# A two-layer encoder trunk on one core: the last gate with tokens on partitions, casts queued ahead of spreads, and five more tiles of u in a borrowed region

## The chip, the core and the metric

The kernel runs on one core of one Trainium2 chip. The core has a matrix engine (TensorE, PE in the views, its weight loads PEld), a vector engine (VectorE, DVE), a scalar engine (ScalarE, ACT), GpSimd (POOL), and SyncE (SP), whose queue issues nearly all transfers. The metric is the device time of one execution in microseconds; the kernel counts as changed if its median moves by more than the measurement can tell.

## What is computed

The input is x, 256 tokens of 1024 features, with two layers. Each layer has a mixer (layer 0: Mamba-2 SSD, layer 1: retention), an expert network of 128 x 128 experts (PEER), and a gated per-layer input. A final RMS norm ends it. The last parts, cut from the reference:

```
h = h + peer_ffn(rms_norm(h, ffn_norm[i]), peer_w_q[i], peer_keys[i], peer_u[i], peer_v[i])
g = jax.nn.sigmoid(rms_norm(h, ple_norm[i]) @ ple_gate[i])
h = h + g * (p[i] @ ple_proj[i])
...
return rms_norm(h, final_norm)
```

In `peer_ffn` every token picks, per head, 16 of the experts by two top-16 searches over 128 keys each; a picked expert's row of u is multiplied with the token, passed through gelu, weighted by a softmax gate and multiplied with its row of v. The kernel computes the products for all 16384 experts densely and multiplies by a gate matrix that is zero where an expert was not picked.

## The kernel before

**Activations and weights.** The residual is kept as `hT`, features on partitions, tokens along the free axis, eight chunks of 128 features (`hch`). Products are made in a split form: a weight tile of 128 x 1024 is loaded into a `raw` buffer (four of them, `raws`), cast by ScalarE into `wh` (lines 136 and 532), and the rest is subtracted into `wl` by VectorE or GpSimd (139, 535); `wh` and `wl` have two buffers each. Activations are split the same way into X tiles. A product is then three passes: wh with the high part, wh with the low part, wl with the high part.

**The weight pipeline.** `makers` is the list of all weight tiles in order. `begin()` issues the transfer of the next one; `prepare()` emits its cast and, unless `late`, its subtraction; `get()` hands out the tile for this step, prepares the next and begins one more. `ahead()` prepares a tile early, leaving its subtraction to the next `get()`. Whatever is emitted later on an engine runs later there: each engine works its queue in the order of emission.

**A dense product.** `dense` goes over eight k-steps of 128 input features; in each it takes a tile, lets the stream bring its activations up to date (`Stream.before`: gain copies by ScalarE, line 332, low parts by VectorE, line 337), emits 24 matmuls of 256 tokens (line 206) and then `fill`s in pieces of other work, as many as the plan of the step says. With `ends=2` the last two k-steps are done bank by bank (`close`, line 221), so that the four banks of PSUM end one after the other. The norm's division is applied to the product: squares on ScalarE (`q`, `Q`, line 349) are added on GpSimd (351, 353); `t` sums them by a matmul with ones (256), a root is taken on VectorE and GpSimd (263, 265), a diagonal made (275), and `s` spreads it over the partitions by two matmuls (282), copied by ScalarE (361). The plans FIRST_SSD, FIRST_RET, FIRST_Q and FIRST_PLE say after which k-step each of these letters is emitted.

**Retention.** Projections, then scores, mixing and a group norm per head, whose pieces stand in RET_ORDER (q: squares, b: sum and diagonal, c: spread and scaling); RET_GATE says how many pieces follow each k-step of the two gate projections. RET_LO lists the tiles whose subtraction GpSimd does.

**PEER.** Two query projections (the second one's subtractions on GpSimd), with eight small transfers of the normed activations after each of the first two steps (`q_move`), from which the X tiles for u are split (`q_fill`). Then 128 tiles of u: each is loaded as four transfers into a row buffer, transposed by VectorE in 32 x 32 blocks (527), cast and split, and multiplied in 24 matmuls (1289, 1290, 1293). The row buffer is one of four slots at offset 16384 of the region `H` that will later hold the experts' activations, as long as i < UEND, and a `raw` buffer after that; the transposed tile is always a `raw` buffer. During the first 60 tiles VectorE also does the selection (`pump`). From the tile where the selection ends, the gate matrix is built for four tokens at a time, 64 groups: `g_hot` makes one-hots on VectorE (1195, 1197), `g_lo` a low part on ScalarE (1203), `g_mm` multiplies them (1209), `g_apply` stores or multiplies the result into H (1219, 1223). `g_slot`, once per tile, emits the matmuls of two ready groups, the one-hots of a next group (two where `since % 8 == 0` and it lags) and the low parts. After the 128 tiles of u, 128 tiles of v are multiplied with H, now with H as the stationary operand and 512 features as the moving one (1315); `peer` ends with the transposes of the result into the residual and the projection of p (1353), evacuated by ScalarE (1357).

**The last stage.** `ple(1, ...)` makes the gate product, divides (364), tanh (1408), multiplies (1384) and adds (1388) into `hT`; `turned_out` transposes 16 chunks back to tokens on partitions (1398), squares and sums them (1401), and the end of `trunk` takes the root (1468 to 1470), scales (1475) and stores four pieces (1476):

```
for j in range(2):
    for tb in range(2):
        o = raws.tile([P, D], F32, name="raw")[:, :512]
        c = slice(512 * j, 512 * j + 512)
        dve.scalar_tensor_tensor(o, ot[2 * j + tb], v[:, 1, tb:tb + 1], gfin[:, c], op0=OP.mult, op1=OP.mult)
        (sp, act)[tb].dma_start(out[0, tb * P:(tb + 1) * P, c], o)
```

## Time and profile before

| | |
|---|---|
| median of three executions | 2146.82 us (2146.73 to 2147.22) |
| the profiled execution | 2147.86 us, its span 2145.3 us |
| mean granted TensorE clock | 0.996 |
| busy share of the span | PE 98%, PEld 91%, DVE 73%, ACT 57%, POOL 36% |
| transfers | 370.24 MB, mean 173 GB/s |
| query projections, tiles of u, tiles of v, layer 1 | about 1288, 1340 and 1750 us from the span's start to the start of each |
| last matmul of the last gate | 2131.75 us |

The span runs from the first to the last instruction; the execution's own time is 2.56 us longer. In the views, "L206" is line 206 of the kernel; `out<-in` names what is written and read; times are microseconds from the span's start, then the duration. A bracket at a row's end is the idle time of the engine before it and what ended it. Matmul durations overlap.

### The profile page before, as it was taken

How to read it: one execution, taken by the hardware profiler on the slowest of the kernel's cores; microseconds unless marked ns; L12 is line 12 of the kernel's file. 1: busy time of each engine (PE TensorE's matmuls, PEld its weight loads, DVE VectorE, ACT ScalarE, POOL GpSimd, SP SyncE). 2: the span in 40 equal slices, each digit the busy share in tenths (PEclk: the TensorE clock that was granted, in tenths of full speed). 3: DMA queues.
4: the chain of work that ended last, by engine and by line, in shares of the span. 5: the costliest groups of instructions: out<-in, count | busy, mean ns of one | idle time of the engine just before them, and what ended most of it. 6: DMA issues, size and time to landing. Idle time of an engine off the chain costs nothing.

```text
span 2145.3 us, 39601 instructions
## 1 busy us (share of the span) xinstructions
PE 2112.3 (98%) x15013; PEld 1959.3 (91%) x15013; DVE 1559.6 (73%) x2645; ACT 1218.8 (57%) x2136; POOL 772.1 (36%) x359
## 2 busy tenths in 40 slices
PE   8999999999999999999999999999999999999997
PEld 8999999999999888888898999999999998888887
DVE  7787688979998555555695457888799975555556
ACT  5675444558887444444554444445688864444445
POOL 0001378876776000000143215788767740000001
PEclk9999999999999999999999999999999999999999
DMA  6424687645555655666655456765555565555553
GB/s 199 147 90 130 206 195 188 175 131 156 156 157 170 199 192 193 194 195 191 217 156 179 121 176 186 189 186 138 161 155 158 152 186 194 196 193 191 195 191 118
DMA packets 219574, 370.24 MB, mean 173 GB/s; under 512 B 24240, under 2 KB 163192, under 8 KB 219384
## 3 DMA queue, kind: packets, MB, share of 16 engines
q1 hardware_dynamic: 218920, 366.93, 57.4%
q8 instruction: 117, 1.92, 0.4%
q10 hardware_dynamic: 464, 0.79, 0.1%
q14 instruction: 73, 0.60, 0.1%
HBM read 364.48 MB, written 1.05 MB: 170 GB/s over the span
## 4 chain that ended last, share of the span: by engine, by line
PE 44%; DVE 2%; issue 1%; POOL 1%; ACT 1%; DMA 1%; SPq 0%; DVEq 0%; POOLq 0%; ACTq 0%
PE ps L1315 16%; PE ps L206 7%; PE m L1289 5%; PE m L1293 5%; PE m L1290 5%; PE ps L913 2%; PE g L1209 1%; DMA raw<-in_peer_u 1%; PE g L1017 0%; DVE wl L139 0%; POOL wl L139 0%; DVE raw L527 0%; PE g L865 0%; POOL wl L535 0%; SPq L524 0%
## 5 line engine op out<-in xcount | busy, mean ns | idle before, releaser
L139 DVE TENSOR_TENSOR wl<-raw,wh 128x1024 fp32r<-128x1024 f32 x404 | 503.6, 1248 | 397.2 <-ACT wh L136 396.9
L136 ACT CAST wh<-raw 128x1024 fp32r<-128x1024 f32 x428 | 449.4, 1052 | 470.5 <-PE ps L1315 358.7
L535 POOL TENSOR_TENSOR wl<-raw,wh 128x1024 fp32r<-128x1024 f32 x256 | 618.1, 2415 | 203.3 <-ACT wh L532 189.2
L1289 PE MATMUL m<-X,wh 128*128 128x256 f32 x2048 | 508.7, 286 | 1.3 <-ACT wh L532 1.3
L1315 PE MATMUL ps<-wh,X 128*128 128x512 f32 x2048 | 507.1, 389 | 0.0
L1290 PE MATMUL m<-X,wh 128*128 128x256 f32 x2048 | 502.3, 283 | 0.0
L1315 PEld LDWEIGHTS ps<-wh,X 128*128 128x128 f32 x2048 | 384.1, 188 | 79.6
L1289 PEld LDWEIGHTS m<-X,wh 128*128 128x128 f32 x2048 | 392.5, 192 | 2.6 <-ACT wh L532 2.3
L1290 PEld LDWEIGHTS m<-X,wh 128*128 128x128 f32 x2048 | 392.7, 192 | 0.0
L206 PE MATMUL ps<-X,wh 128*128 128x256 f32 x2368 | 330.3, 288 | 3.3 <-ACT wh L136 1.2
L351 POOL TENSOR_TENSOR arena<-arena 128x512 f32<-128x512 f32 x15 | 24.1, 1610 | 809.6 <-ACT arena L349 800.5
L206 PEld LDWEIGHTS ps<-X,wh 128*128 128x128 f32 x2368 | 302.0, 194 | 9.5 <-DVE arena L364 1.9
L1293 PE MATMUL m<-X,wl 128*128 128x256 f32 x2048 | 288.1, 283 | 2.1 <-POOL wl L535 2.1
L532 ACT CAST wh<-raw 128x1024 fp32r<-128x1024 f32 x256 | 266.4, 1041 | 25.4 <-DVE raw L527 16.6
L1315 PE MATMUL ps<-wl,X 128*128 128x512 f32 x1024 | 274.7, 389 | 0.0
L1293 PEld LDWEIGHTS m<-X,wl 128*128 128x128 f32 x2048 | 264.0, 192 | 3.8 <-POOL wl L535 3.5
L1315 PEld LDWEIGHTS ps<-wl,X 128*128 128x128 f32 x1024 | 192.2, 188 | 40.0
L1229 ACT ACTIVATE arena<-m 128x256 f32<-128x256 f32 (+15 forms) x248 | 82.0, 331 | 229.6 <-PE m L1293 229.4
L527 DVE STREAM_TRANSPOSE raw<-raw 128x1024 f32<-128x1024 f32 x144 | 179.0, 1243 | 42.4 <-DMA raw<-in_peer_u 31.0
L206 PE MATMUL ps<-X,wl 128*128 128x256 f32 x1184 | 175.1, 284 | 2.3 <-POOL wl L139 1.3
L527 DVE STREAM_TRANSPOSE raw<-arena 128x1024 f32<-128x1024 f32 x112 | 138.0, 1235 | 30.1 <-POOL wl L535 22.3
L206 PEld LDWEIGHTS ps<-X,wl 128*128 128x128 f32 x1184 | 156.4, 192 | 3.6 <-POOL wl L139 1.9
(269 smaller groups left out, 1969.4 us busy)
## 6 DMA issues: line engine op xcount, KB each, us to landing
raw<-in_peer_v SPq DMA_DIRECT2D x256, 512.0 KB, 4.3
raw<-in_peer_u SPq DMA_DIRECT2D x576, 128.0 KB, 3.1
arena<-in_peer_u SPq DMA_DIRECT2D x448, 128.0 KB, 3.2
raw<-in_ret_w_in SPq DMA_DIRECT2D x48, 512.0 KB, 3.9
raw<-in_ssd_w_in SPq DMA_DIRECT2D x41, 512.0 KB, 3.7
raw<-in_peer_w_q SPq DMA_DIRECT2D x32, 512.0 KB, 4.3
raw<-in_ssd_w_out SPq DMA_DIRECT2D x16, 512.0 KB, 3.8
raw<-in_ple_gate SPq DMA_DIRECT2D x16, 512.0 KB, 4.7
```

The source lines that it names most:

```text
L136: (cast or act.copy)(wh[:, :n], r[:, :n])
L139: (eng or dve).tensor_sub(wl[:, :n], r[:, :n], wh[:, :n].bitcast(F32))
L206: pe.matmul(self.t[n // 2][:, n % 2], w[:, n * P:(n + 1) * P], x, start=st, stop=sp_, skip_group_check=True)
L527: dve.transpose(t.rearrange("p (k b i) -> p b k i", k=8, b=4), r.rearrange("p (b k i) -> p b k i", k=8, b=4))
L532: act.copy(wh, t)
L535: pool.tensor_sub(wl, t, wh.bitcast(F32))
L913: pe.matmul(pss[j], abc[i][0][:, tb * P:(tb + 1) * P], abc[i][1][:, n * 512:(n + 1) * 512], start=kk == 0 and i == 0, stop=kk == 7 and i == 2)
L1229: act.activation(H[:, i, st:], ps[:, st:], AF.Gelu)
L1289: pe.matmul(last, wh[:, s], xh, start=k == 0, stop=False)
L1290: pe.matmul(last, wh[:, s], xl, start=False, stop=False)
L1293: pe.matmul(last, wl[:, s], xh, start=False, stop=k == KD - 1)
L1315: pe.matmul(sums[b], h[:, tb * P:(tb + 1) * P], w[:, n * 512:(n + 1) * 512], start=i == 0 and p == 0, stop=i == P - 1 and p == 2)
```

## The change

1. The last gate, projection and output are written as `ple_last`, with tokens on partitions: the activations are the stationary operand, 512 features the moving one. The residual is transposed within the gate (`turn`, after steps 1 and 2) and p's projection added to it; the norm's root is a scale per partition of the tanh, so there is no spread. The output is scaled by the final root in four pieces.
2. `spread` calls `ahead()` first, and the first step of retention's first projection does so too (`turned`).
3. FIRST_RET moves the letters Q, t, s and the first scaling one step later; RET_GATE moves the last sum of the group norm one step later; RET_LO gives tile 46 to VectorE.
4. The last tile of the second query projection is subtracted by VectorE; the activations for u are split one step earlier.
5. UEND goes from 56 to 61.
6. The second one-hot of a slot is emitted after `g_done`.

```diff
 NEG = -3.0e38
 GS = 4096.0
 PUMP = 1700
-UEND = 56
+UEND = 61
 HPOOL = (0, 1)
...
 RET_ORDER = """
     n0 m0 s1 q0 m1 s2 b0 c0 n1 s3 q1 m2 b1 n3 c1 n2 q2 m3 b2 c2 q3 b3 c3
 """.split()
-RET_GATE = (2, 2, 1, 2, 1, 2, 1, 2, 1, 2, 1, 2, 1, 2, 1, 0)
-RET_LO = (8, 22, 31, 33, 46, 48, 51)
+RET_GATE = (2, 2, 1, 2, 1, 2, 1, 2, 1, 2, 1, 2, 1, 2, 0, 1)
+RET_LO = (8, 22, 31, 33, 48, 51)
 FIRST_SSD = ('aq', 't', 'c', 's', '0', 'h', '1b', 'H')
-FIRST_RET = ('', 'qQ', '', 'cbt', 'das0', '', 'h1', 'H')
+FIRST_RET = ('', 'q', 'Q', 'cb', 't', 'das0', 'h1', 'H')
 FIRST_Q = ('q', 'Q', '', 't', 'sa', 'b', '', '')
 FIRST_PLE = ('', 'q', 'Q', '', 't', 's', '', '')
+FIRST_LAST = ('', 'qa', 'Qb', '', 't', '', '', '')
 HEADS = 8
 TOPK = 16
...
         def __init__(self, col):
             self.col, self.xs, self.n, self.src = col, [], 0, hch
+            self.turned = False
             self.sq, self.rb = view(12288, 4, 512), view(14336, T)
         def gain(self, c):
...
         def before(self, k):
+            if self.turned and not k:
+                ahead()
             while len(self.xs) < KD:
                 self.hi(len(self.xs))
             while self.n < min(k + 3, KD):
...
             self.sums.sum(self.sq[:, 0, :T])
             self.dg = self.sums.diag(D)
+        def roots(self):
+            self.sums = Sums()
+            self.sums.sum(self.sq[:, 0, :T])
+            r = self.sums.root(D)
+            self.rh = small.tile([P, 2], F32, name="rh", bufs=1)
+            dve.tensor_scalar(self.rh, r, 0.5, None, op0=OP.mult)
         def spread(self):
+            ahead()
             act.copy(self.rb, self.sums.spread(self.dg))
         def divide(self, dst, ps):
...
             for k in range(16):
                 weights(a["ret_w_out"][0], 0, D, k, k + 1, eng=pool if 48 + k in RET_LO else None)
         for g in range(2):
-            weights(a["peer_w_q"][l], g * D, (g + 1) * D, eng=pool if g else None)
+            for k in range(KD):
+                weights(a["peer_w_q"][l], g * D, (g + 1) * D, k, k + 1, eng=pool if g and k < KD - 1 else None)
         for i in range(P):
             makers.append(lambda l=l, i=i: u_maker(a["peer_u"][l], i))
         weights(a["peer_v"][l], 0, D, 0, P)
...
             if k < 2:
                 q_move(2 * k)
                 q_move(2 * k + 1)
-            if k in (4, 6):
-                xh, xl = split_x(xm[:, 2 * k - 8:2 * k - 4])
+            if k in (3, 5):
+                xh, xl = split_x(xm[:, 2 * k - 6:2 * k - 2])
                 xp.extend((xh[:, i], xl[:, i]) for i in range(4))
             return 0
...
             return len(gst["ready"]) > 1 or (gst["ready"] and gst["next"] == T // 4 and not gst["hot"])
-        def g_slot(n=1):
+        def g_new():
+            if gst["next"] < T // 4 and not bg and gst["next"] < gst["mms"] + 4:
+                gst["hot"].append((gst["next"], g_hot(gst["next"])))
+                gst["next"] += 1
+        def g_slot():
             if g_due():
                 for b, x in gst["ready"][:2]:
...
                     gst["mms"] += 1
                 gst["ready"] = gst["ready"][2:]
             lo, gst["hot"] = gst["hot"], []
-            while n and gst["next"] < T // 4 and not bg and gst["next"] < gst["mms"] + 4:
-                gst["hot"].append((gst["next"], g_hot(gst["next"])))
-                gst["next"] += 1
-                n -= 1
+            g_new()
             for b, x in lo:
                 g_lo(b, *x)
                 gst["ready"].append((b, x))
...
                     pump(PUMP)
                 else:
                     since += 1
-                g_slot(2 if since % 8 == 0 and T // 4 - gst["next"] > P - 5 - i else 1)
+                g_slot()
                 g_done(i)
+                if since % 8 == 0 and T // 4 - gst["next"] > P - 5 - i:
+                    g_new()
                 if cur is None and not open_():
                     cur = wsplit(0)
             last = mis.tile([P, 512], F32, name="m")[:, :T]
...
                 wh, wl = get()
                 st2 = finish(turned, COL["ple_norm"] + 8 * l)
             for w_, x_ in ((wh, 0), (wh, 1), (wl, 0)):
+                if l:
+                    for j in range(4):
+                        pe.matmul(pq[j], pts[x_][:, kk, j // 2 * P:(j // 2 + 1) * P],
+                                  w_[:, j % 2 * 512:(j % 2 + 1) * 512],
+                                  start=kk == 0 and w_ is wh and x_ == 0, stop=kk == 1 and w_ is wl)
+                    continue
                 for n in range(8):
                     pe.matmul(pq[n // 2][:, (n % 2) * T:(n % 2 + 1) * T], w_[:, n * P:(n + 1) * P], pts[x_][:, kk],
                               start=kk == 0 and w_ is wh and x_ == 0 and n % 2 == 0, stop=kk == 1 and w_ is wl,
...
+    def ple_last(st, pp):
+        pp = pp.rearrange("p (a b) t -> p a (b t)", a=4)
+        g, hp, og, o = (view(i, 4, 512) for i in (2560, 6144, 8192, 24576))
+        gfin, junk = view(16384, D), view(17408, 512)
+        fs = small.tile([P, 2, 2], F32, name="fs", bufs=1)
+        v = small.tile([P, 2, 2], F32, name="r2")
+        sp.dma_start(gfin, a["final_norm"].partition_broadcast(P))
+        def turn(tb):
+            for n in range(2):
+                ps = gps.tile([P, 512], F32, name="g")
+                for c in range(4):
+                    pe.transpose(ps[:, c * P:(c + 1) * P], hch[4 * n + c][:, tb * P:(tb + 1) * P], ident)
+                dve.tensor_add(hp[:, 2 * tb + n], ps, pp[:, 2 * tb + n])
+        sums = [acc.tile([P, 512], F32, name="ps") for _ in range(4)]
+        def mms(j, wh, wl, xh, xl, parts, start, stop):
+            t, n = slice(j // 2 * P, (j // 2 + 1) * P), slice(j % 2 * 512, (j % 2 + 1) * 512)
+            for i in parts:
+                pe.matmul(sums[j], (xh, xl, xh)[i][:, t], (wh, wh, wl)[i][:, n], start=start and i == 0,
+                          stop=stop and i == 2)
+        st.total = st.roots
+        plan = first(st, None, FIRST_LAST, (turn, 0), (turn, 1))
+        for k in range(KD - 2):
+            wh, wl = get()
+            st.before(k)
+            for i in range(3):
+                for j in range(4):
+                    mms(j, wh, wl, *st.xs[k], (i,), k == 0, False)
+            fill(plan(k))
+        steps = [get(k < KD - 1) + st.xs[k] for k in (KD - 2, KD - 1)]
+        for j in range(4):
+            mms(j, *steps[0], range(3), False, False)
+            mms(j, *steps[1], range(3), False, True)
+        def tanh(j):
+            act.activation(g[:, j], sums[j], AF.Tanh, scale=st.rh[:, j // 2:j // 2 + 1])
+        def total(j):
+            dve.tensor_mul(g[:, j], g[:, j], pp[:, j])
+            dve.tensor_add(g[:, j], g[:, j], hp[:, j])
+        def square(j):
+            act.activation(junk, g[:, j], AF.Square, scale=1.0 / 32, accum_out=fs[:, j // 2, j % 2:j % 2 + 1])
+        def gains(j):
+            dve.tensor_mul(og[:, j], g[:, j], gfin[:, j % 2 * 512:(j % 2 + 1) * 512])
+        def root(tb):
+            dve.scalar_tensor_tensor(v[:, 0, tb:tb + 1], fs[:, tb, 0:1], EPS, fs[:, tb, 1:2], op0=OP.add, op1=OP.add)
+            pool.tensor_tensor(v[:, 1, tb:tb + 1], v[:, 0, tb:tb + 1], mhalf[:, :1], op=OP.pow)
+        def store(j, eng, queue):
+            r = v[:, 1, j // 2:j // 2 + 1]
+            if eng is act:
+                act.activation(o[:, j], og[:, j], AF.Copy, scale=r)
+            else:
+                dve.scalar_tensor_tensor(o[:, j], g[:, j], r, gfin[:, j % 2 * 512:(j % 2 + 1) * 512],
+                                         op0=OP.mult, op1=OP.mult)
+            queue.dma_start(out[0, j // 2 * P:(j // 2 + 1) * P, j % 2 * 512:(j % 2 + 1) * 512], o[:, j])
+        assert D == 1024
+        tanh(0)
+        tanh(1)
+        total(0)
+        square(0)
+        tanh(2)
+        total(1)
+        square(1)
+        tanh(3)
+        total(2)
+        root(0)
+        square(2)
+        total(3)
+        square(3)
+        gains(0)
+        store(0, act, sp)
+        root(1)
+        gains(2)
+        gains(3)
+        store(2, act, act)
+        store(1, dve, sp)
+        store(3, act, sp)
     state = [st0]
...
+    ple_last(*state)
```

## Rows read from the trace of the kernel before

**Rows 1.** The page, part 1: busy time, share of the span, instructions.
```profile
PE 2112.3 (98%) x15013; PEld 1959.3 (91%) x15013; DVE 1559.6 (73%) x2645; ACT 1218.8 (57%) x2136; POOL 772.1 (36%) x359
```
**Rows 2.** Chain that ended last, 2090 to 2146: start, duration, what, instructions.
```profile
2090.77 8.23 PE ps L1315 x36
...
2101.87 1.76 PE ps L1341 x16
...
2106.51 14.39 PE ps L206 x120
```
**Rows 3.** TensorE's waits, whole span: for whom, total, times, longest.
```profile
PE m L256 <- POOL arena L293: 1.8, 1, 1.8
PE g L1209 <- DVE arena L1223: 1.7, 2, 0.8
...
PE ps L221 <- ACT wh L136: 1.4, 2, 0.7
PE ps L206 <- POOL wl L139: 1.3, 2, 0.7
...
PE ps L206 <- ACT wh L136: 1.2, 1, 1.2
PE ps L221 <- DVE wl L139: 1.0, 2, 0.5
...
PE m L256 <- POOL arena L353: 0.8, 1, 0.8
```
**Rows 4.** Timeline of the last stage, 2122 to 2146.
```profile
2131.48 0.63 ACT L1408 ACTIVATE arena<-arena 128x512 f32<-128x512 f32 x1 [0.81 <-DVE arena L364]
...
2131.75 0.40 PE L221 MATMUL ps<-X,wl 128*128 128x256 f32 x2
...
2137.62 0.38 ACT L1401 ACTIVATE arena<-m 128x256 f32<-128x256 f32 x1
...
2138.57 0.70 POOL L1470 TENSOR_TENSOR r<-r,mhalf 128x2 f32<-128x2 f32 x1 [4.71 <-DVE r L1469]
...
2140.63 1.40 DVE L1475 SCALAR_TENSOR_TENSOR raw<-m,r,arena 128x512 f32<-128x512 f32 x2
2140.75 1.67 ACTq L1476 DMA_DIRECT2D out<-raw  x2
```
**Rows 5.** Timeline of retention's second gate projection, 1210 to 1246.
```profile
1229.37 2.40 POOL L139 TENSOR_TENSOR wl<-raw,wh 128x1024 fp32r<-128x1024 f32 x1 [1.74 <-ACT wh L136]
...
1234.83 0.61 PE L256 MATMUL m<-ones,arena 128*128 128x1 f32 x4 [1.79 <-POOL arena L293]
```
**Rows 6.** Window behind that wait: each engine's busy time, then granted clock, DMA share, GB/s.
```profile
1235.80:1239.20 3.40, 3.40 (x18) 3.40 (x18) 1.04 (x1) 1.77 (x4) 1.66 (x2) 0.50 0.21 81
```
**Rows 7.** Timeline of retention's first projection: its evacuations.
```profile
1101.46 2.48 DVE L364 TENSOR_TENSOR arena<-ps,arena 128x512 f32<-128x512 f32 x4
```
**Rows 8.** Timeline of layer 1's second query projection, 1305 to 1352.
```profile
1329.47 8.12 POOL L139 TENSOR_TENSOR wl<-raw,wh 128x1024 fp32r<-128x1024 f32 x3 [1.39 <-ACT wh L136]
...
1330.38 2.60 DVE L195 TENSOR_TENSOR X<-arena,X 128x1024 fp32r<-128x1024 f32 x1 [6.08 <-DMA arena<-in_peer_u]
```
**Rows 9.** Chain of waits among layer 1's tiles of u, 1500 to 1565.
```profile
1502.50 4.55 DMA raw<-in_peer_u
...
1515.52 3.19 DMA raw<-in_peer_u
...
1544.20 0.93 PE g L1209 x16
```
**Rows 10.** Timeline of TensorE: low-part matmuls of tiles 54, 62 (layer 0), 54, 63 (layer 1).
```profile
444.56 1.12 PE L1293 MATMUL m<-X,wl 128*128 128x256 f32 x8
...
471.24 1.12 PE L1293 MATMUL m<-X,wl 128*128 128x256 f32 x8
...
1501.97 1.12 PE L1293 MATMUL m<-X,wl 128*128 128x256 f32 x8
...
1533.47 1.12 PE L1293 MATMUL m<-X,wl 128*128 128x256 f32 x8
```

More of the change, by code (lines that the diff above doesn't have):

```diff
@@ L1416, in g_evac @@
                 gated(2)
[L1418 to L1421 removed]
+        keys = view(30464, 4, 512)
+        for c4 in range(4):
+            key_load(1, c4, keys[:, c4])
         dense(st, g_evac, first(st, None, FIRST_PLE), ends=2)
[L1423 to L1436 removed]
@@ L1437, in ple @@
-        ot = [pool_.tile([P, 512], F32, name=n_) for pool_, n_ in ((gps, "g"), (gps, "g"), (mis, "m"), (mis, "m"))]
+        tiles = [pool_.tile([P, 512], F32, name=n_) for pool_, n_ in ((gps, "g"), (gps, "g"), (mis, "m"), (mis, "m"))]
+        for c4 in range(4):
+            key_turn(keys[:, c4], tiles[c4])
+        st2.turned = True
+        st2.copies = [(key_copy, c4, tiles[c4]) for c4 in range(4)]
+        st2.lo(0)
+        ready.append(ready.pop()())
+        st2.lo(1)
+        prepare(True)
@@ L1438, in ple @@
+        ready.append(ready.pop()())
         added(2)
-        turned_out(0)
         gated(3)
         added(3)
-        for b in range(1, 4):
-            turned_out(b)
-        return ot, fs, gfin
+        return st2
+    def ple_last(st, pp):
[72 more added lines that the diff above has]
+        store(3, act, sp)
```

50 lines of the change are left out of this document (4 added, 46 removed).

## The prediction

> **What bounds the kernel now.** I read the page first: TensorE is busy 98% of the span [rows 1], so the sum of its matmuls is a floor, and a change can win only in fewer TensorE microseconds, in its waits, or behind its last matmul. The chain of waits gives the price of a matmul by the distance of successive starts, not by the listed duration, which overlaps the next one: 120 matmuls of 256 columns in 14.39 us are 0.120 us each, 36 of 512 columns in 8.23 us are 0.229, a transpose is 1.76/16 = 0.11 [rows 2]. Third, TensorE's own waits [rows 3]: each is under 2 us, and the seven listed, 9.2 us in all, sit where this diff works. Last, the timeline of the end [rows 4]: the last matmul ends at 2131.75 + 0.40 = 2132.15 and the span at 2145.3, so 13.15 us pass with hardly any TensorE work.
>
> **The change, part by part.** Times are against the profiled execution, 2147.86 us (span 2145.3 and 2.56 around it); the median of the three runs is 1.04 lower.
>
> (a) *Last gate and projection.* The gate's 24 matmuls of 256 columns per k-step become 12 of 512: 8 x (24 x 0.1199 - 12 x 0.2286) = 1.08 us less; the projection's 48 become 24, 0.27 less; four spread matmuls at 0.11 go, 0.45 less [rows 2]. The 16 transposes that ran behind the gate now run inside it, 1.76 more. TensorE's stream is therefore level (-0.05), and narrow against wide is worth little. What counts is the end. In the close, TensorE waited for the last weight tile's cast and then its subtraction, 1.4 and 1.0 us over the two gates [rows 3] plus the restart of the pipeline, 1.53 a gate by the starts. In the last gate no spread copy stands ahead of that cast any more, but the cast still needs the buffer of the tile two before, and the subtraction queues on VectorE behind the wait for the root. I put the wait at 0.9, so -0.6.
>
> Behind the last matmul I walk the new order, with t = 0 at its end and durations of [rows 4]. Banks finish 6 x 0.229 = 1.37 us apart, so only the fourth counts. ScalarE is still squaring the second part until 0.2; tanh of the fourth takes 0.63, to 0.9. VectorE's two passes per part (1.40 for two) keep pace with the banks but finish the third part at 1.05; the fourth is done at 2.4. Its square with the sum read out is 0.38 for 256 columns plus the read; I estimate 0.75 for 512, to 3.2. A small VectorE sum, the power on GpSimd (0.70) and hand-overs reach 4.2. Two scaled copies on ScalarE at 0.63 end at 5.5, VectorE's own store beside them. From the last multiply's end before (2140.63 + 1.40 = 2142.03) to the end of the span were 3.27 us; two transfers queued on SP add 0.4. Sum: 9.1 instead of 13.15, -4.0. Part (a): **-4.7**; bounds -6 (no wait in the close, tail 8.3) and -2 (VectorE's four added 0.7 us adds push a weight subtraction late by 1, and the tail loses another 1.5).
>
> (b) *Cast ahead of the spread, gate of layer 0.* The same close, but the spread stays. With the cast ahead of it, the last cast starts when its buffer is free, 1.9 us into step 5, and the subtraction is late by about 0.45 instead of 1.53 in all: **-1.1**, bounds -1.5 and 0. At the query projections the same move finds no wait to remove: 0.
>
> (c) *Retention's first projection.* Step 2 waited 1.2 us (1.4 by the starts) for a cast queued behind four gain copies that wait for the residual; the sum of squares waited 0.8 for GpSimd [rows 3]. `ahead()` puts the cast first, and the sum moves to step 4, where the squares are long done. That makes TensorE up to 2.3 us earlier, but the scaled copies start at the end of step 5 instead of 4, and then VectorE, which needs 2.48 us for the four evacuations alone [rows 7], is late instead: TensorE waits for its banks some 0.8 longer. **-1.5**; bounds -2.3 and +0.5.
>
> (d) *Retention's gates.* GpSimd does a weight subtraction of 2.40 us, then two passes over the squares, and TensorE waits 1.8 for them [rows 3, 5]. Right behind that wait the granted clock reads 0.50, that is 1.2 GHz, for 3.4 us [rows 6]: 18 matmuls ran in it, where at 2.4 GHz 3.4 / 0.12 = 28 would, so it cost 10 x 0.12 = 1.2 more. The diff gives that subtraction to VectorE and lets the sum run a step later, after the evacuations; either is enough. Given back: the diagonal then waits for the power while ScalarE's queue holds the next cast, by my walk 0.65 us at the second output tile. The wait is 1.95 by the starts: -1.95 - 1.2 + 0.65 = **-2.5**; bounds -3.2 and +1 (the power behind the next GpSimd subtraction, 2.4 us, with a slow clock after it).
>
> (e) *Last tile of the second query projection on VectorE; splits of the moved activations one step earlier.* TensorE waits 1.3 us in two places, 0.8 each by the starts, for a GpSimd subtraction [rows 3], the last of three that took 8.12 instead of 7.2 us while VectorE ran its two-tensor subtractions, the first in 2.60 [rows 8]. With the splits earlier and the last subtraction on VectorE it is ready about 1 us early: **-1.6** for both layers; bounds -1.7 and +0.5. The row shows the two engines slowing each other, and 2.60 still fits.
> The Trainium skill (SBUF — State Buffer, "SBUF: two separate sides") says that VectorE with two SBUF inputs and GpSimd exclude each other on a shared port pair for a whole instruction. The slowing in the row agrees in kind; by the rule in full, the moved subtraction could stand behind a whole GpSimd one.
>
> (f) *Rows of u in the activations' region up to tile 60.* From tile 56 on, rows and transposed rows share four buffers, and the chain runs through them: transfers of 4.55 and 3.19 us, 13.02 us from the first to the one four tiles on [rows 9], 6.5 us per two tiles. TensorE wants 48 x 0.12 = 5.76 per two. From the subtraction matmuls of tile 54 to those of tile 62 in layer 0 are 26.68 us, eight tiles are 23.04 and the eight selection transposes about 0.77: 2.9 lost. In layer 1, tile 54 to 63, 31.50 - 25.92 - 0.77 - 0.93 (one group of gate matmuls) = 3.9 lost [rows 9, 10]. Moved to tile 61, the switch meets a VectorE that has done the selection, and TensorE then needs 5.76 + 0.93 = 6.69 per two tiles, more than 6.5. The first switch hiccup (about 0.9, as at tile 57) and some lateness of the first one-hots (0.3 to 1.3) remain: I keep 1.6 a layer, so (2.9 - 1.6) + (3.9 - 1.6) = **-3.6**; bounds -6.8 and +1.5 (the hiccup meets the first gate matmuls and a slow clock follows).
>
> (g) *Second one-hot after the activations are stored.* Counting the slots by the code, the old order issues two groups of gate matmuls in adjacent tiles (71 and 72), and TensorE waits there for the store of the first, 1.7 in two layers [rows 3], 2.0 by the starts. In the new order they are always two tiles apart, and the last group falls one tile later, at 125. **-2.0**; bounds -2.0 and 0.
>
> Sum: -4.7 - 1.1 - 1.5 - 2.5 - 1.6 - 3.6 - 2.0 = -17.0 us: 2130.9 for a profiled execution, **2129.8** for the median.
>
> **The rivals.**
> *Half comes back.* TensorE reaches every later point earlier, while VectorE and DMA do not; the next operand is then late. Places: the switch at tile 61 keeps its 6.8 us (+3.6), retention's first projection wins nothing (+1.5), the close and tail give 2 instead of 4.7 (+2.7): 2129.8 + 7.8 = 2137.6. For: (c) and (f) are bounded by VectorE and transfers, not by TensorE. Against: the tail is a chain whose every link is in [rows 4].
> *The port excludes.* Then the moved subtraction waits up to 2.4 us [rows 5] and ends 3.6 after its cast, after the moment TensorE wants it: (e) gives nothing, 2131.4. Against: 2.60 in [rows 8]. The Trainium skill's page on SBUF, cited under (e), is where this rule stands.
> *More.* No wait is left in (a) to (g): all lower bounds, -22.6, 2124.
> *The change doesn't do what it says.* `ahead()` asks for a weight buffer that step 0 still reads, so the cast may just wait at another place, and (f) may only move its stall; if (a) wins 2 and nothing else stays, 2144.8: no measurable change.
> *Slower.* One mechanism: the two-tile loop through the shared buffers. From tile 61 to 125 it is the only supply; if TensorE, no longer delayed before, stays in step with transfers of the 4.55 kind instead of 3.19, a pair takes about 7.2 us instead of 6.69 and 64 pairs lose 33 us: 2163. It decides from 0.27 us a pair. Against: the same loop feeds tiles 72 to 125 today, and TensorE's wait list has no such row [rows 3].
>
> **Numbers.** The forecast as summed, 2125 to 2134: 0.55; the port: 0.08 (inside that span too); half back, 2134 to 2142: 0.25; more, below 2125: 0.05; no change: 0.04; slower: 0.03. The range 2124.5 to 2137.5 leaves out the two last, the end of the best case and the outer part of "half back", about 2 in 10; the likeliest case alone spans 2125 to 2134. A measurement of this kernel can tell about 0.2%, 4.3 us, from no change: faster 0.93, same 0.04, slower 0.03.
>
> **What would show it.** TensorE's waits lose the rows on the GpSimd squares, on the GpSimd subtraction and on the gate store; no stretch at 0.50 between the start and the end besides the early one in layer 0's mixer; tiles 56 to 60 start 2.88 us apart; from the last matmul to the end 9 us. It is wrong if the tail is longer than 11 us, if tiles 61 to 64 lose more than 3 us a layer, or if retention's output projection starts with a new wait above 2 us.

## The result, and the profile after

The changed kernel takes 2130.77 us, the median of four runs (2128.72 to 2131.07), against 2146.78 us for the kernel before, also of four. The ratio is 0.9923 with an interval of 0.9911 to 0.9935. The forecast was 2129.8 us with a range of 2124.5 to 2137.5. The profiled execution took 2130.51 us with a span of 2128.5, that is 16.8 us less span than the one shown before, where the working had 17.0.

The page, part 1, of the changed kernel: TensorE has 124 fewer instructions and 8.3 us less busy time than in [rows 1], and its busy share rises to 99%.

```profile
PE 2104.0 (99%) x14889; PEld 1948.7 (92%) x14889; DVE 1558.7 (73%) x2649; ACT 1220.2 (57%) x2132; POOL 761.5 (36%) x355
```

TensorE's waits in the changed kernel (for whom; total, times, longest):

```profile
PE ps L207 <- POOL wl L140: 1.4, 4, 0.4
PE ps L207 <- DVE wl L140: 1.3, 4, 0.6
...
PE ps L207 <- DVE arena L377: 0.9, 1, 0.9
...
PE ps L207 <- ACT wh L137: 0.4, 1, 0.4
PE ps L1470 <- DVE wl L140: 0.4, 1, 0.4
```

Gone from [rows 3] are both rows on GpSimd's squares, the row on the gate store and the close's wait for a cast. The row on GpSimd's weight subtraction is as large as before, 1.4 instead of 1.3, in four places instead of two; and a row on VectorE's evacuations (DVE arena L377) is new.

The end of the changed kernel, from the last bank on (timeline):

```profile
2118.42 0.39 PE L1470 MATMUL ps<-wl,X 128*128 128x512 f32 x1
...
2118.99 0.67 ACT L1489 ACTIVATE arena<-ps,rh 128x512 f32<-128x512 f32 x1
...
2119.82 0.97 POOL L1504 TENSOR_TENSOR r<-r,mhalf 128x1 f32<-128x1 f32 x1 [8.86 <-DVE r L1503]
...
2120.42 0.69 DVE L1493 TENSOR_TENSOR arena<-arena 128x512 f32<-128x512 f32 x1
...
2121.21 0.63 ACT L1497 ACTIVATE arena<-arena 128x512 f32<-128x512 f32 x1 [0.72 <-DVE arena L1493]
...
2122.20 0.94 POOL L1504 TENSOR_TENSOR r<-r,mhalf 128x1 f32<-128x1 f32 x1 [1.41 <-DVE r L1503]
...
2123.17 0.72 ACT L1509 ACTIVATE arena<-arena,r 128x512 f32<-128x512 f32 x1 [0.63 <-POOL r L1504]
...
2123.92 0.38 ACTq L1513 DMA_DIRECT2D out<-arena  x1
2124.35 0.72 ACT L1509 ACTIVATE arena<-arena,r 128x512 f32<-128x512 f32 x1 [0.46 <-DVE arena L1511]
```

The last matmul ends at 2118.81 and the span at 2128.5: 9.7 us where [rows 4] had 13.15. The chain of the last bank can be followed downwards: tanh, VectorE's second pass, the square, the power on GpSimd (0.94 us, not 0.70), two scaled copies with ScalarE's issue of a transfer (ACTq) between them, the last transfer.

Where the 16.8 us came from, by the starts of the matmuls that bound each stage in the two traces, beside what the experiments below gave back when a part was undone:

| part | forecast | trace, before to after | undone alone |
|---|---|---|---|
| (a) last stage | -4.7 | -4.36 | layout +3.27 |
| (b) layer 0's gate, close | -1.1 | -1.38 | +1.37 |
| (c) retention, first projection | -1.5 | -0.77 | early cast +1.43; order +0.14 |
| (d) retention's gates | -2.5 | -3.20 | sum's place +1.29; subtraction +1.00 |
| (e) query projection, two layers | -1.6 | +0.70 | -0.70 |
| (f) rows of u | -3.6 | -5.17 (tiles 54 to 64) | +3.72 |
| (g) second one-hot | -2.0 | -2.05 (from tile 64 on) | +2.05 |
| outside the edits | 0 | -0.66 | |

The last column compares single profiles with the one shown here. In (d) and (f) it holds some luck: each of (d)'s two numbers can be 0.82 us too large, because the profile shown here happens to have a short power on GpSimd (last section), and (f)'s is 1.0 smaller for where a transfer landed (u56, below).

### The profile page after: what moved, and what is told of

Same layout as the page of the kernel before. It is cut to its first block, busy times and chain, and to the rows that moved or that the text cites. A ratio compares the mean times of both kernels' runs of the same rounds, so it can differ in the third digit from the quotient of the medians.

```text
span 2128.5 us, 39345 instructions
## 1 busy us (share of the span) xinstructions
PE 2104.0 (99%) x14889; PEld 1948.7 (92%) x14889; DVE 1558.7 (73%) x2649; ACT 1220.2 (57%) x2132; POOL 761.5 (36%) x355
## 5 line engine op out<-in xcount | busy, mean ns | idle before, releaser
L140 DVE TENSOR_TENSOR wl<-raw,wh 128x1024 fp32r<-128x1024 f32 x407 | 510.2, 1255 | 396.8 <-ACT wh L137 396.1
L207 PE MATMUL ps<-X,wh 128*128 128x256 f32 x2272 | 315.0, 287 | 3.9 <-DVE arena L377 0.9
L207 PEld LDWEIGHTS ps<-X,wh 128*128 128x128 f32 x2272 | 287.7, 192 | 10.0 <-issue 2.2
L1243 ACT ACTIVATE arena<-m 128x256 f32<-128x256 f32 (+16 forms) x250 | 82.9, 332 | 240.2 <-PE m L1312 240.0
L540 DVE STREAM_TRANSPOSE raw<-raw 128x1024 f32<-128x1024 f32 x134 | 166.5, 1243 | 36.7 <-POOL wl L548 18.7
L207 PE MATMUL ps<-X,wl 128*128 128x256 f32 x1136 | 168.1, 284 | 2.8 <-POOL wl L140 1.4
L540 DVE STREAM_TRANSPOSE raw<-arena 128x1024 f32<-128x1024 f32 x122 | 149.8, 1232 | 26.8 <-POOL wl L548 21.1
L207 PEld LDWEIGHTS ps<-X,wl 128*128 128x128 f32 x1136 | 149.7, 192 | 4.9 <-DVE wl L140 2.4
```

The source lines that it names most:

```text
L140: (eng or dve).tensor_sub(wl[:, :n], r[:, :n], wh[:, :n].bitcast(F32))
L207: pe.matmul(self.t[n // 2][:, n % 2], w[:, n * P:(n + 1) * P], x, start=st, stop=sp_, skip_group_check=True)
L540: dve.transpose(t.rearrange("p (k b i) -> p b k i", k=8, b=4), r.rearrange("p (b k i) -> p b k i", k=8, b=4))
L1243: act.activation(H[:, i, st:], ps[:, st:], AF.Gelu)
```

## The experiments

Ten kernels ran once each; their single times spread by some 2 us (the section on the hardware says why), so each was read by stages: the distance of the same two matmuls in its trace and in the changed kernel's, which agrees to some 0.1 us in most stages that an edit doesn't touch. The exceptions are the kernel's start and layer 0's mixer, tile 62 of u in layer 1, and the places that the last section names. Two versions meant to be better were timed in five rounds.

**u56: the switch of u's rows back.**

```diff
-UEND = 61
+UEND = 56
```

> The changed kernel with the rows of u sent back to their own buffers from the 57th tile on, as before; nothing else is touched. Theory: the longer use of the activations' region is worth what the trace of the changed kernel lacks between the 54th and the 64th tile, 2.76 us in the first layer and 2.41 in the second, less the 0.9 to 1.1 that comes back later in the same loop only if it belongs to this part: so 4.0 to 5.2 us longer, near 2135.5. Rival, the transfers' lateness is only put off and TensorE waits for the second one-hot group instead: under 1 us.

2135.36 us. Tiles 54 to 64 took 2.43 us longer in layer 0 and 1.29 in layer 1, and nothing came back behind them: 3.72, a little under the 4.0 to 5.2 expected, far from the rival's 1. TensorE's waits show the two rows that the late rows of u make; the changed kernel has 0.6 (2 times) in the first and nothing in the second.

```profile
PE m L1312 <- POOL wl L548: 2.2, 7, 0.3
...
PE m L1308 <- ACT wh L545: 1.1, 2, 0.7
```

Layer 1 loses less at tile 62, where the first gate group is multiplied: it takes 5.16 us in the changed kernel and 4.13 in this one, but 5.23 in the kernel before, which switches at tile 56 as well. The first one-hots stand on VectorE behind a transpose that waits for a transfer of u. It starts 1.2 us ahead of tile 62 in this run, 0.2 in the changed kernel and 0.1 in the kernel before (VectorE's timelines: changed, u56, before):

```profile
1514.81 1.25 DVE L540 STREAM_TRANSPOSE raw<-raw 128x1024 f32<-128x1024 f32 x1 [2.22 <-DMA raw<-in_peer_u]
...
1519.04 1.25 DVE L540 STREAM_TRANSPOSE raw<-raw 128x1024 f32<-128x1024 f32 x1 [1.29 <-DMA raw<-in_peer_u]
...
1526.15 1.25 DVE L527 STREAM_TRANSPOSE raw<-raw 128x1024 f32<-128x1024 f32 x1 [2.44 <-DMA raw<-in_peer_u]
```

In the runs that leave UEND at 61 tile 62 takes 4.58 to 5.26 there. So 1.0 us of layer 1's smaller loss is where one transfer landed; whether a second run of u56 would show it too isn't known.

**q_pool, split_late, q_old: the query projection's two edits, one by one and together.**

```diff
 q_pool, q_old:
-weights(..., k, k + 1, eng=pool if g and k < KD - 1 else None)
+weights(..., k, k + 1, eng=pool if g else None)
 split_late, q_old:
-if k in (3, 5):
-    xh, xl = split_x(xm[:, 2 * k - 6:2 * k - 2])
+if k in (4, 6):
+    xh, xl = split_x(xm[:, 2 * k - 8:2 * k - 4])
```

> The changed kernel with the subtraction of the last tile of the query's weights on GpSimd again; the two splits of the input stay one step early. Theory (VectorE's subtraction of 3.17 us stands beside GpSimd's two of 5.96, each longer than alone, and so the move buys nothing): the query projection of the second layer, from its first step to the first tile of u, within 0.6 us of the changed kernel's, either sign. Rival, the prediction's term: it takes 1 us or more longer, in each of the two layers, about 2 us in all.

> The changed kernel with the two splits of the input after the steps before's had them; the last tile of the query's weights stays with VectorE. Theory: the early split's copy on ScalarE stands ahead of the cast of the next weights and makes GpSimd idle 2.33 us, so the two new waits of 0.36 and 0.32 us go and the projection of the second layer gets 0.5 to 1.1 us shorter; the wait for the activations that the early split was for comes back at up to 0.5 at the next step. Rival, the order of ScalarE's queue has no part in it: the same 0.36 and 0.32 stay.

> The changed kernel with both edits of the query projection undone. Theory (port and queue give back what the edits win): the projection is within 0.4 us of the changed kernel's in each layer, by the two traces already at hand 0.24 shorter in the second and 0.2 shorter in the first. Rival, the prediction's term: 1.6 us longer over both layers.

2134.54, 2136.85 and 2131.54 us. Layer 0, against the changed kernel, up to the start of step 7, then to the first tile of u, then to tile 54: q_pool 0, +0.92, -0.11; split_late -1.12, 0, +2.30; q_old -1.14, +0.91, -0.13. Layer 1 has the same but for split_late's last number, 3.46: behind the wait the granted clock reads 0.5 there, that is 1.2 GHz, for 3.4 us. Against q_old, the old pair, in layer 0 the early splits alone therefore cost 1.2 us, the moved subtraction alone 1.5, and both together 0.36 (0.34 in layer 1). q_pool came out nearer to the rival, q_old as the theory had it, and split_late as neither: the two waits went, but a larger one came. The timeline of the changed kernel, layer 0, shows the first half:

```profile
272.34 5.96 POOL L140 TENSOR_TENSOR wl<-raw,wh 128x1024 fp32r<-128x1024 f32 x2 [2.34 <-ACT wh L137]
...
274.90 1.22 PE L207 MATMUL ps<-X,wl 128*128 128x256 f32 x8 [0.36 <-POOL wl L140]
...
276.21 3.18 DVE L140 TENSOR_TENSOR wl<-raw,wh 128x1024 fp32r<-128x1024 f32 x1 [0.16 <-issue]
...
278.36 1.22 PE L207 MATMUL ps<-X,wl 128*128 128x256 f32 x8 [0.33 <-POOL wl L140]
```

GpSimd idles 2.34 us for a cast that stands behind the early split on ScalarE, and then needs 5.96 for two subtractions of 2.4. With the splits late, VectorE's half of the second split stands behind the moved subtraction, a transpose and a piece of the selection, and tile 0 of u waits for it (timeline of split_late):

```profile
282.32 2.45 DVE L196 TENSOR_TENSOR X<-arena,X 128x1024 fp32r<-128x1024 f32 x1
...
284.83 0.39 PE L1309 MATMUL m<-X,wh 128*128 128x256 f32 x1 [1.77 <-DVE X L196]
```

**g_old: both one-hot groups in one slot again.**

```diff
...
-                g_slot()
+                g_slot(2 if since % 8 == 0 and T // 4 - gst["next"] > P - 5 - i else 1)
                 g_done(i)
-                if since % 8 == 0 and T // 4 - gst["next"] > P - 5 - i:
-                    g_new()
```

> The changed kernel with the old slot of the gate groups, which issues the second one-hot group in the same slot as the first and ahead of the store. Theory (two groups of gate matmuls fall in adjacent tiles and TensorE waits for the store of the first): tiles 64 to 76 take 1.8 us longer in each layer, 0.7 to 0.9 comes back later in the loop because the last group falls one tile earlier, so about 2.0 in all; tiles 54 to 64 unchanged. Rival, the order also spares tiles 54 to 64 (the undone region of u explained only 2.43 and 1.29 of the 2.76 and 2.41 there): 0.3 and 1.1 more, 3.4 in all.

2133.21 us. Tiles 64 to 76 took 2.22 and 1.83 us longer, 0.90 came back behind them in each layer, and tiles 54 to 64 were 0.02 and 0.20 shorter: +1.32 and +0.73, in all 2.05. The wait of [rows 3] is back (2.0 in two places, the longest 1.2):

```profile
PE g L1223 <- DVE arena L1237: 2.0, 2, 1.2
```

The rival is out. But u56 and g_old together make 5.77 of the 7.22 us by which the traces differ there. Of the other 1.45, 1.3 is tile 62 of layer 1 again: 5.23 us in the kernel before and 5.16 in the changed one, but 4.13 in u56 and 4.95 in g_old. Both undone together was not run.

**gate_old and lo46: retention's two gate edits, one by one.**

```diff
 gate_old, end of RET_GATE:
-2, 1, 2, 0, 1)
+2, 1, 2, 1, 0)
 lo46:
-RET_LO = (8, 22, 31, 33, 48, 51)
+RET_LO = (8, 22, 31, 33, 46, 48, 51)
```

> The changed kernel with the sum of a head's squares back ahead of the last step of the third gate part; the subtraction of that stage's weight tile stays with VectorE. Prediction's theory, either of the two edits is enough: the last step and the one before together within 0.5 us of the changed kernel's. Rival, only the sum's place matters, since the squares' own two passes on GpSimd end too late anyway: 1.5 to 3.2 us longer, with TensorE waiting for GpSimd's second pass over the squares.

> The changed kernel with that stage's weight subtraction on GpSimd again, and the sum one step later as changed. Prediction's theory, either edit is enough: within 0.5 us of the changed kernel's, from the second gate part to the output projection. Rival, the squares that stand behind GpSimd's 2.4 us are still late a step later: 1 to 2 us longer, and the wait stands at the sum's matmuls behind the last step.

2131.23 and 2133.17 us. From the start of the second gate projection to the output projection's second tile gate_old took 1.29 us longer and lo46 1.00, of 3.20 for both. That misses the 0.5 of the theory, and neither rival's wait is there. Either edit is enough against the wait for the squares, which neither kernel has; whether it is enough for the rest these two runs can't say. The power on GpSimd behind the sum takes 1.72 in gate_old and 1.68 in lo46, against 0.70 in the profile that they are compared with, and of the ten profiles that have both edits and are else alike here, six have the long power too and are 0.82 longer for it (last section). Measured against those, gate_old would be some 0.5 longer and lo46 0.2. In gate_old another wait takes the place of that for the squares (TensorE's waits, then GpSimd's timeline):

```profile
PE ps L207 <- ACT arena L937: 1.4, 1, 1.4
```

```profile
1225.44 0.74 POOL L294 TENSOR_TENSOR arena<-arena 128x256 f32<-128x256 f32 x1
1227.41 1.72 POOL L266 TENSOR_TENSOR r<-r,mhalf 128x2 f32<-128x2 f32 x1 [1.23 <-DVE r L264]
```

The squares are done in time; the power takes 1.72 and ends at 1229.13, and only then do ScalarE's two diagonal copies and the cast behind them start, with the four evacuations queued behind both.

**no_ahead: without the early casts.**

```diff
         def spread(self):
-            ahead()
...
-            if self.turned and not k:
-                ahead()
```

> The changed kernel without the two calls that cast the next weight tile ahead (ahead of the spread, and ahead of the gain copies of retention's first step). Theory, these calls alone make the gains at both places: the close of layer 0's gate gets 1.4 us longer, retention's steps 0 to 2 get 1.3 longer, and of the latter at most 0.9 comes back at the banks of the first projection, where TensorE waits 0.88 for VectorE's evacuations: 1.8 to 2.7 in all. Rival, the changed order of the squares, sum and spread makes the gain and the early cast none: under 0.5.

2135.91 us. Layer 0's close got 1.37 us longer, retention's steps 0 to 4 1.58, of which 0.15 came back; nothing came back at the banks, where TensorE waits as long as in the changed kernel. (Behind that wait this run has 3.4 us at 1.2 GHz, which cost 1.5 and are left out here; the last section tells of them.) That makes 2.8 us, a little above the theory's range, since almost nothing is given back.

**first_old_split45: retention's first order as before; both splits one step apart.**

```diff
-FIRST_RET = ('', 'q', 'Q', 'cb', 't', 'das0', 'h1', 'H')
+FIRST_RET = ('', 'qQ', '', 'cbt', 'das0', '', 'h1', 'H')
...
-if k in (3, 5):
-    xh, xl = split_x(xm[:, 2 * k - 6:2 * k - 2])
+if k in (4, 5):
+    xh, xl = split_x(xm[:, 4 * k - 16:4 * k - 12])
```

> Two edits in two stages that are read apart. One: the order of the squares, sum and scaled copies in retention's first projection as before, with the early cast kept. Theory (the new order removes the wait for GpSimd's squares but sets the scaled copies ahead of the evacuations, so TensorE waits 0.88 at its banks): steps 2 to 4 get 1.4 us longer, steps 4 to 7 0.6 to 0.7 shorter and the close 1.0 to 1.2 shorter, within 0.5 of the changed kernel in sum. Rival, the prediction's -1.5 for this place came half from the order: 0.7 or more longer. Two: the splits of the second layer's and the first layer's moved activations after steps 4 and 5 instead of 3 and 5. Theory (the first early split pushes a weight cast back and GpSimd with it; only the second has to be early, since the first tile of u waited 1.77 us for its VectorE half when it came late): the last steps lose the waits of 0.36 and 0.33, 1.1 us less in each layer, and the first tile of u has no new wait. Rival, either of the two splits pushes the cast: no gain, or the old waits at another step.

2129.61 us. The order: steps 2 to 4 took 2.36 us longer, steps 4 to 7 0.74 shorter, the close 1.22 and the next part 0.26 shorter, so 0.14 in sum: on top of the early cast the new order buys next to nothing. The two lean on each other: against the kernel before, the early cast without the order wins 0.63 here, the order without the early cast loses 0.66 (no_ahead), both together win 0.77. The splits: 1.14 less at steps 5 and 6, 0.77 more at step 7 and 0.36 more in u's first tile: 0 in each layer. The waits moved on by a step. Its timeline, layer 1:

```profile
1319.56 5.76 POOL L140 TENSOR_TENSOR wl<-raw,wh 128x1024 fp32r<-128x1024 f32 x2 [1.39 <-ACT wh L137]
...
1320.46 5.94 DVE L196 TENSOR_TENSOR X<-arena,X 128x1024 fp32r<-128x1024 f32 x2 [6.09 <-DMA arena<-in_peer_u]
...
1327.59 0.50 PE L207 MATMUL ps<-X,wl 128*128 128x256 f32 x2 [0.52 <-DVE wl L140]
...
1332.37 1.22 PE L1312 MATMUL m<-X,wl 128*128 128x256 f32 x8 [0.21 <-POOL wl L548]
```

Two VectorE subtractions that take 1.21 each alone (best2, below) need 5.94 us beside two of GpSimd's, which need 5.76 instead of 4.8.

**late1_last_old: the second scaled copies behind the evacuations; the last stage in the old layout.**

```diff
-FIRST_RET = ('', 'q', 'Q', 'cb', 't', 'das0', 'h1', 'H')
+FIRST_RET = ('', 'q', 'Q', 'cb', 't', 'das0', 'h', '1H')
...
-ple_last(*state)
+(before's projection of p and last gate, its transposes behind the gate, its four stores)
```

> Two edits in two stages that are read apart. One: in retention's first projection the second four scaled copies come behind the evacuations of the first part instead of ahead of them. Theory (the four copies, 1.65 us on VectorE, are what makes the banks late): the wait of 0.88 at the start of the next part goes, 0.9 to 1.0 us less, and no wait appears at that part's fifth step, where these copies are first read. Rival, the evacuations are late of themselves: the wait stays at 0.8 or more. Two: the last gate and projection in the old layout, within the changed kernel. Theory: the last stage takes 4.3 us longer, 0.9 of it ahead of the last matmul and 3.4 behind, as the two traces differ. Rival, the early cast alone would have won the close of the old layout: at most 3.4 longer, all of it behind the last matmul.

2133.09 us. One: the wait of 0.88 at the banks went (-1.02), and 2.21 us came back in the next part, from step 1 on. In the changed kernel the copies stand ahead of the evacuations (timeline, VectorE and TensorE):

```profile
1093.78 1.65 DVE L383 SCALAR_TENSOR_TENSOR arena<-hT,par,m 128x256 f32<-128x256 f32 x4
1095.35 2.48 DVE L377 TENSOR_TENSOR arena<-ps,arena 128x512 f32<-128x512 f32 x4
...
1096.18 3.15 PE L207 MATMUL ps<-X,wh 128*128 128x256 f32 x16 [0.88 <-DVE arena L377]
```

In this kernel they come behind, and ScalarE's split of them, which stands ahead of the next weight casts, waits for them (timeline, ScalarE and TensorE):

```profile
1096.84 1.05 ACT L195 CAST X<-arena 128x1024 fp32r<-128x1024 f32 x1 [4.30 <-DVE arena L383]
1097.80 2.00 ACT L137 CAST wh<-raw 128x1024 fp32r<-128x1024 f32 x2
...
1098.89 2.18 PE L207 MATMUL ps<-X,wh 128*128 128x256 f32 x16 [1.17 <-ACT wh L137]
```

Two: the last stage took 3.27 us longer, not 4.3. With the early cast the old layout's last matmul comes 31.91 us behind the last of the products with v, against 33.26 before and 32.29 in the new layout; behind it 13.4 us pass instead of 9.7. The rival held: the early cast alone wins the close, and all that the layout wins lies behind the last matmul.

**best1: three edits meant to mend (c), (d) and (e).** It has the splits of first_old_split45, the order of late1_last_old, and:

```diff
         def gn_sum(h):
+            if h == 3:
+                ahead()
```

> The changed kernel with three edits: the splits after steps 4 and 5, the second four scaled copies behind the evacuations, and, in retention's output projection, the cast of the second weight tile ahead of the last head's diagonal copies on ScalarE. Theory: 1.1 us less in each of the two query projections, 0.9 to 1.0 at retention's first projection, 0.5 at the second tile of the output projection, and with these waits gone the slow-clock stretches behind them that some runs show (1.5 and 0.8 us): 3.7 us under the changed kernel's profile, near 2126.8, ratio to before near 0.991. Rival, waits only move on: above 2129.5.

2134.36 us, the median of five (2131.2 to 2138.62), ratio to before 0.9943 with an interval of 0.993 to 0.9957: not better than the changed kernel. The first two edits did what they did above. (The 0.8 that the expectation calls a slow clock is the long power of the last section.) The third removed the wait at the second output tile (-0.62), and 3.64 us came back two tiles on, where VectorE's weight subtraction comes 0.08 us behind one of GpSimd's (timeline):

```profile
1238.33 2.39 POOL L140 TENSOR_TENSOR wl<-raw,wh 128x1024 fp32r<-128x1024 f32 x1 [5.56 <-PE ps L207]
1238.41 3.39 DVE L140 TENSOR_TENSOR wl<-raw,wh 128x1024 fp32r<-128x1024 f32 x1
```

It lasts 3.39 us, GpSimd's 2.39 and about its own; TensorE waits 1.74 for it, and from 1243.5 to 1247 the granted clock reads 0.69, with a part at 1.2 GHz.

**best2: no GpSimd in the last steps of the query projection; the old order of (c).**

```diff
-weights(..., k, k + 1, eng=pool if g and k < KD - 1 else None)
+weights(..., k, k + 1, eng=pool if g and k < 5 else None)
```

with the splits and the `FIRST_RET` of first_old_split45.

> The changed kernel with two edits. One: in the second query projection the last three weight subtractions, not the last alone, go to VectorE, and the splits come after steps 4 and 5. Theory, from the runs before (GpSimd's two subtractions took 5.76 us and VectorE's two split halves beside them 5.94, where VectorE takes 1.21 for one alone and idles 6.09 us just before): the engines exclude each other over the whole instruction, so five VectorE subtractions in a row without GpSimd take about 1.2 each, all are in time, and each layer gets 1.0 to 1.2 us shorter between the fifth step and the first tile of u, with no new wait in that tile. Rival, the cost is in the number of subtractions and not in the two engines at once: VectorE's five are late and the waits stand at the sixth and seventh step. Two: retention's first projection in the old order of squares, sum and copies, which cost 0.14 us in the run that had it and had no slow-clock stretch of 1.5 us behind the banks. In all: a profile near 2127 to 2128 and a median of five 1 to 3 us under the changed kernel's; if the rival holds, within 1 us of it or above.

2131.24 us, the median of five (2130.73 to 2132.7), ratio 0.9933 with an interval of 0.992 to 0.9947: the changed kernel's time. VectorE's timeline in layer 1, and TensorE's wait:

```profile
1320.65 1.23 DVE L140 TENSOR_TENSOR wl<-raw,wh 128x1024 fp32r<-128x1024 f32 x1 [7.47 <-ACT wh L137]
1321.80 0.48 DVE L1041 MAX8 arena<-arena 128x8 f32<-128x128 f32 x2
...
1324.14 1.21 DVE L196 TENSOR_TENSOR X<-arena,X 128x1024 fp32r<-128x1024 f32 x1
1325.27 1.22 DVE L140 TENSOR_TENSOR wl<-raw,wh 128x1024 fp32r<-128x1024 f32 x1
1326.40 1.22 DVE L196 TENSOR_TENSOR X<-arena,X 128x1024 fp32r<-128x1024 f32 x1
1327.54 1.22 DVE L140 TENSOR_TENSOR wl<-raw,wh 128x1024 fp32r<-128x1024 f32 x1
...
1328.81 0.50 PE L207 MATMUL ps<-X,wl 128*128 128x256 f32 x2 [0.59 <-DVE wl L140]
```

Without GpSimd each of the five takes 1.21 to 1.23 us: the duration is settled by the neighbour. The stage still won nothing (-1.12, +0.84, +0.41 a layer), since 2.3 us of the selection, from 1321.80 to 1324.14, stand between the first and the second, and the fifth ends at 1328.76 where TensorE wanted it 0.59 earlier.

## Why the forecast was right, and where it was not

The sum was right to 1 us. By its steps:

(a) The mechanism was right; two terms were off, against each other. The gain ahead of the last matmul is 0.97 (33.26 to 32.29) instead of 0.65: the wait for the last tile's subtraction, put at 0.9, is 0.6 by the starts (0.4 in the wait list). The tail is 9.7 us and not 9.1. Up to the end of the power it runs nearly as walked (4.3 instead of 4.2, though the power takes 0.94). Then the two scaled copies take 0.72 each instead of 0.63, and 0.46 passes between them, in which ScalarE issues the transfer of the copy just made (0.38; VectorE, which the row names, had been done since 2123.98): they end at 6.3 and not 5.5. The last transfer takes 0.3 less than was put down for it. late1_last_old corrects the reason: the layout doesn't win in the close but loses 0.4 there, most of it in a wait for the last subtraction that is 0.25 longer by the starts; the early cast wins 1.35. "What counts is the end" held: the layout's gain is all in the tail.

(b) -1.38 for -1.1, and no_ahead gives the same 1.37 back. By the starts the close waited 1.74 before and waits 0.36 now, for the last subtraction.

(c) The term that was mis-sized is what is given back. TensorE is 2.24 us earlier, as worked out, but then loses 1.47 and not 0.8, because four scaled copies of 1.65 us stand ahead of the evacuations as well. The other way round the loss is larger still, 2.21 (late1_last_old). And the new order, added to the early cast, is worth 0.14, so nearly all that remains of (c) needs the early cast.

(d) -3.20 for -2.5. The wait for the squares and the slow clock behind it went. The 0.65 at the second output tile was 0.54 in the changed kernel's profile and 1.4 in six others with the same code there, for the reason in the last section; against those (d) gives 2.4, so 0.8 of the 3.20 is the luck of one profile. "Either is enough" was right for the wait; for the rest it stays open, since either edit alone is 1.0 to 1.3 longer than the profile with the short power and 0.2 to 0.5 longer than those with the long one, an estimate from the 0.82 between them.

(e) This step failed: -1.6 forecast, +0.70 measured. Its first half was right: the last tile's wait for GpSimd went, some 0.9 us a layer at step 7. What the step put at nothing was the earlier split. Its copy on ScalarE pushes a weight cast back, and two new waits of 0.52 and 0.49 by the starts stand at steps 5 and 6. "2.60 still fits" was the wrong reading of [rows 8]: GpSimd's first subtraction, 2.4 us from 1329.47, ends at 1331.87, and the 2.60 from 1330.38 end 1.11 behind that, which fits a subtraction of about 1.2 that had to wait better than one that was slowed; the moved one took 3.18. The rival that the port excludes came near the outcome, nothing from (e), but not by its own path: the moved subtraction was long, yet in time, and TensorE waits instead for GpSimd's two, which start late behind the early split and take 5.96.
The Trainium skill (SBUF — State Buffer, "SBUF: two separate sides") states this exclusion, for VectorE instructions with two SBUF inputs against GpSimd. The runs agree: 5.94 us for two beside GpSimd and 1.21 to 1.23 for each without it; from 1319.56 to 1326.40 are 6.84 us, a little under the 7.2 that the four subtractions take one after the other.

(f) By the two traces 5.17 for 3.6, 2.76 and 2.41 a layer for 1.3 and 2.3; undone alone 3.72, for the reason under u56. The wait and its cause were read rightly; the term that was mis-sized is the 1.6 a layer that was to remain. Tiles 56 to 60 start 2.88 apart, as forecast, and no hiccup of 0.9 is left at the switch: tile 60 is 0.75 longer in both layers, but those are the eight selection transposes, which the forecast had counted by themselves. What remains is the first one-hots' lateness at tile 62, 0.3 in layer 0 and 1.35 in layer 1 (4.11 and 5.16 against 2.88 + 0.93).

(g) 2.05 for 2.0. The wait and its cause were read rightly.

That the sum came out within 1 us owes much to chance. (e) and (c) fell short by 3.0 us; (d) gave 0.7 and (f) with (g) 1.6 more than forecast, and 0.66 came from outside the edits. The shown profile of the changed kernel also has none of the three losses, 3.8 us together, that the last section finds in other profiles. One sum of the forecast is wrong without consequence: its lower bounds add up to -23.5, not -22.6, so the best case is near 2123.3.

## What to carry to other kernels

Price a VectorE instruction by what GpSimd does at that moment: the same subtraction took 1.22 us and 3.18 us here. But the neighbour was not all: with GpSimd out of the way (best2) the stage still won nothing, since other work stood in VectorE's queue. When an edit puts an operation earlier in a queue, list what it now stands ahead of: with (e) a wait of 0.8 at one step went, and two of 0.5 came at the steps ahead of it. And judge a part by undoing it alone and reading its own stage, since the whole kernel's time moves by 2 us for other reasons; and look first whether the profile that it is compared with was lucky in that very stage.

## What the runs showed of the hardware that was not expected

The power on GpSimd, two numbers a row, races VectorE. In the changed kernel it starts first and takes 0.70 us (timeline, retention's last sum):

```profile
1230.92 0.70 POOL L266 TENSOR_TENSOR r<-r,mhalf 128x2 f32<-128x2 f32 x1 [1.15 <-DVE r L264]
1231.07 1.23 DVE L905 TENSOR_TENSOR arena<-arena 128x1024 f32<-128x1024 f32 x1 [0.23 <-issue]
...
1234.38 2.17 PE L207 MATMUL ps<-X,wh 128*128 128x256 f32 x16 [0.38 <-ACT wh L137]
```

In q_pool, with the same code there, the multiply comes 0.16 us ahead of the power, which takes 1.61, and TensorE waits 0.82 longer:

```profile
1233.09 1.22 DVE L905 TENSOR_TENSOR arena<-arena 128x1024 f32<-128x1024 f32 x1
1233.25 1.61 POOL L266 TENSOR_TENSOR r<-r,mhalf 128x2 f32<-128x2 f32 x1 [1.15 <-DVE r L264]
...
1237.53 1.70 PE L207 MATMUL ps<-X,wh 128*128 128x256 f32 x12 [1.20 <-ACT wh L137]
```

Of ten profiles with the same code there, six show 1.61 and four 0.70.

The granted clock behind one and the same wait also differs from run to run. Behind the 0.88 at the banks of (c), the window's clock (the number behind the engines' busy times) is 1.00, that is 2.4 GHz, in the changed kernel and 0.66 in q_pool, with stretches at 1.2 GHz in it:

```profile
1098.00:1103.00 5.00, 5.00 (x42) 5.00 (x43) 5.00 (x9) 1.80 (x2) 1.49 (x1) 1.00 0.50 159
```

```profile
1098.00:1103.00 5.00, 4.81 (x25) 4.52 (x25) 4.58 (x9) 1.41 (x2) 0.58 (x1) 0.66 0.49 145
```

It costs 1.49 us, in four of the eight profiles that have this code, and 1.50 in no_ahead, which differs there by the early cast alone; a like stretch of 1.5 us behind a wait of 0.94 near 79 us stands in eight of all fourteen profiles, that of the kernel before among them and that of the changed kernel not. These three places are larger together than the 2 us or so by which single runs of a kernel differ; the 0.66 outside the edits is the stretch near 79 us, 1.53, less 0.9 lost at other places ahead of the first edit. What decides them was not found. The four with the slow stretch at the banks (u56, q_pool, split_late, q_old) ran on one chip, and g_old, gate_old and lo46, which don't have it, on another; but no_ahead ran on that other chip and has it, and near 79 us each of the two chips shows both kinds. In split_late the granted clock reads 0.95 from the start to the end; outside its stretches at 0.5 the matmuls start as far apart as in the changed kernel, so this reading cost nothing.
